# Attention statistics kept as minus the maximum, and value products of four attention steps in one burst

## The chip, the cores and the metric

The kernel runs on one core of a Trainium2 chip. The metric is the device time of one execution in microseconds (us); the figure for a kernel is the median of its runs. One execution is also profiled: its span runs from the first to the last instruction.

## The reference

Two requests, a prompt of 1024 tokens and a sample of 512, pass through two layers with the same weights, all in float32. Layer 0 (A) attends in three dilated groups (dilation 1, 4, 16) and merges them by their softmax denominators; layer 1 (B) attends in a band of 128 keys to either side, with 16 query heads over 4 key heads and a sink logit per head. Cut to what the change touches:

```python
def _dilated_group(q, k, v, dil, n_side, slopes):        # layer A, once per group
    s = einsum(qb, kb) * Dh ** -0.5
    s = where(valid, s - slopes * dil * abs(rel), -inf)
    m = max(s, -1); p = exp(s - m); den = sum(p, -1)
    o = einsum(p / den, vb); lse = m + log(den)
    ...
wts = softmax(stack(lses), axis=0)                       # merge of the groups
...
m = maximum(max(s, -1), sink)                            # layer B
p = exp(s - m); den = sum(p, -1) + exp(sink - m)
```

Before and after the attention stand the large products `u @ w_in` and `(att * silu(z)) @ w_out`, an adaLN modulation and a layer norm.

## The kernel before

**Order of the work.** The program goes through a list of projection chunks: layer A of the sample, layer A of the prompt, output layer 0, layer B of the sample, layer B of the prompt, output layer 1. A projection group is 24 matmuls into one PSUM tile `a` (line 364; every operand is split in a high and a low part, so three products for each of eight k-blocks). Inside `run_plan`, after every 4 matmuls of 512 columns or 8 of 256, `slot()` is called. `spread(tasks, slots)` makes a queue of small tasks that are handed out evenly over so many slots. So the attention of head pair `p` is threaded, task by task, between the projection matmuls of the chunks that follow. The engines take their instructions in the order in which they were written.

**An attention step** is one block of 128 queries for the two heads of a pair. It has three tasks:

- `att_a`: the score matmuls into two PSUM tiles `s` (lines 557, 558, 562; the pool has two buffers, so a step's scores wait until the step before has been read). VectorE then adds the bias, scales, and takes the row maximum in one custom instruction per head (line 412, which also writes its accumulator into the statistics `st`). One more VectorE instruction writes `nm`, the two maxima negated (line 416), and ScalarE takes the exponentials with bias `nm` and the row sums (line 419).
- `att_b`: TensorE transposes of the probabilities `P` into PSUM tiles `t` (line 430), copied to SBUF tiles `PT` by ScalarE for head 0 (line 438) and VectorE for head 1 (line 440).
- `att_c`: for a pair of steps, the value products into PSUM tile `o` (line 458): each matmul has 64 output columns of the array, head 0 in rows 0 to 63 of `o` and head 1 in 64 to 127. Then one `copy` of 128x256 (helper at lines 160 and 162, ScalarE and VectorE in turn) out of `o`. The pool of `o` has one buffer.

`pipeline` writes the tasks of a pair's 4 or 8 steps: for each i, `att_b` of step i-2, `att_a` of step i, and on even i from 4 on `att_c` of the pair that began at step i-4. Layer A runs this twice per head pair (dilations 4 and 16 together, then dilation 1), layer B once.

**Merge.** `merge_tasks` (lines 731 to 748) turns the maxima and sums in `st` into factors, in seven small VectorE instructions and one exponential. In layer B the other side of the merge is the sink logits `sinks`.

**GpSimd** (POOL) splits the streamed weights into high and low part (lines 334 and 341), for all stages.

Of the kernel before, what the change touches and what calls it, by code (L numbers as in the profile page):

```python
# [10 lines left out]
F32 = mybir.dt.float32  # L11
F32R = mybir.dt.float32r
AF = mybir.ActivationFunctionType
ALU = mybir.AluOpType
# [61 lines left out]
def trunk(ctx: ExitStack, tc: tile.TileContext, x_p, x_s, c_p, c_s, w_mod, b_mod, ln_g, ln_b,  # L76
          w_in_a, w_out_a, w_in_b, w_out_b, sink_b, pat_d, id_d, y_p, y_s):
    nc = tc.nc
    PSUM = bass.MemoryType.PSUM
    const = ctx.enter_context(tc.tile_pool(name="const", bufs=1))  # L80
    wk = ctx.enter_context(tc.tile_pool(name="wk", bufs=2))
# [5 lines left out]
    ps_o = ctx.enter_context(tc.tile_pool(name="ps_o", bufs=1, space=PSUM))  # L87
# [14 lines left out]
    sinks = const.tile([128, NH], F32, name="sinks")  # L102
# [23 lines left out]
    def after(n, f):  # L126
        delayed.append((now[0] + n, f))
# [11 lines left out]
    def spread(tasks, slots):  # L139

        q = Queue(tasks, slots)
        queues.append(q)
        return q
# [13 lines left out]
    def copy(out, in_):  # L157
        turn[0] ^= 1
        if turn[0]:
            nc.scalar.activation(out, in_, AF.Copy)  # L160
        else:
            nc.vector.tensor_copy(out, in_)  # L162
# [31 lines left out]
    def load_mod(l, third, k):  # L194
        t = slabs.get()
        nc.sync.dma_start(t, w_mod[l, k * 128:(k + 1) * 128, third * D:(third + 1) * D])
        return t

    def mod_mm(ts):
        a = ps_t.tile([128, 512], F32, tag="t", name="t")  # L200
        for i in range(NK // 2):
            for par in range(2):
                for c in range(2):
                    g = 2 * c + par
                    k = 2 * i + par
                    nc.tensor.matmul(a[32 * g:32 * g + 32, :], lhsT=sc[:, k, :],  # L206
                                     rhs=ts[k][:, c * 512:(c + 1) * 512],
                                     start=(i == 0), stop=(i == NK // 2 - 1),
                                     tile_position=(0, 32 * g))
        slabs.put(*ts)  # L210
        m = wk.tile([128, 512], F32, tag="stg", name="modrow")
        nc.scalar.activation(m, a, AF.Copy)
        return m
# [189 lines left out]

    def att_a(s):
        ss = []
        nm = wk.tile([128, 2], F32, tag="nm", name="nm", bufs=4)
        s.P = []
        ts = [ps_s.tile([128, 384], F32, tag="s", name="s") for _ in range(2)]
        s.scores(ts)
        for h, t in enumerate(ts):  # L410
            p = wk.tile([128, 384], F32, tag="P", name="P", bufs=4)
            nc.vector.tensor_tensor_reduce(  # L412
                out=p[:, :s.n], in0=t[:, :s.n], in1=s.bias(h), op0=ALU.add, op1=ALU.max,
                scale=0.125, scalar=-3e38, accum_out=s.st[:, s.b, h, 0:1])
            s.P.append(p)
        nc.vector.tensor_scalar(nm, s.st[:, s.b, :, 0], -1.0, None, ALU.mult)  # L416
        for h in range(2):
            p = s.P[h]
            nc.scalar.activation(p[:, :s.n], p[:, :s.n], AF.Exp, bias=nm[:, h:h + 1],  # L419
                                 accum_out=s.st[:, s.b, h, 1:2])  # L420

    def att_b(s):
# [17 lines left out]
                    nc.vector.tensor_copy(pt[r0:r0 + n, i:j], t[r0:r0 + n, i:j])  # L440
                i = j

    def att_c(pair):

        o = ps_o.tile([128, 256], F32, tag="o", name="o")
        a, b = pair.steps
        at = {k[4]: i for i, k in enumerate(b.keys)}
        both = [(i, at[k[4]]) for i, k in enumerate(a.keys) if k[4] in at]
        ops = [(a.keys[i], slice(i, 4 + j, 3 + j - i), slice(0, 256)) for i, j in both]
        for n, s in enumerate(pair.steps):  # L450
            ops += [(k, slice(3 * n + i, 3 * n + i + 1), slice(128 * n, 128 * n + 128)) for i, k in enumerate(s.keys)
                    if i not in [x[n] for x in both]]
        fresh = [True, True]
        for m, ((_, n, r0, v, _), blocks, cs) in enumerate(ops):
            steps = range(cs.start // 128, cs.stop // 128)
            stop = not any(both or o2[2] == cs for o2 in ops[m + 1:])
            for h in range(2):
                nc.tensor.matmul(o[64 * h:64 * h + 64, cs], lhsT=v(h)[r0:r0 + n, :],  # L458
                                 rhs=pair.PT[h][r0:r0 + n, blocks, :], start=fresh[steps[0]], stop=stop)
            for x in steps:  # L460
                fresh[x] = False
        out = a.into.rearrange("p (b q) -> p b q", q=128)[:, a.b:b.b + 1:b.b - a.b]
        copy(out, o.rearrange("p (b q) -> p b q", q=128))

    class Pair:
        pass
# [1 line left out]
    def pipeline(steps):  # L468
        tasks = []
        n = len(steps)  # L470
        for i, s in enumerate(steps):
            s.first = i % 2 == 0
            if s.first:
                s.pair = Pair()
                s.pair.steps = steps[i:i + 2]
            else:
                s.pair = steps[i - 1].pair
        for i in range(n + 3):
            if 2 <= i < n + 2:
                tasks.append(lambda s=steps[i - 2]: att_b(s))  # L480
            if i < n:
                tasks.append(lambda s=steps[i]: att_a(s))
            elif i < n + 2:
                tasks.append(None)
            if i >= 4 and i % 2 == 0:
                tasks.append(lambda s=steps[i - 4]: att_c(s.pair))
        return tasks + [None]

    def load_pat(c0, n, o=0):
# [228 lines left out]
    def merge_tasks(p, r, l, st, use=None):  # L718
# [4 lines left out]
        def m1():  # L723
            a = st["st1"]
            M = wk.tile([128, nb, 2], F32, tag="M", name="M", bufs=1)
            st["dd"] = wk.tile([128, 2, nb, 2], F32, tag="dd", name="dd", bufs=1)
            if l == 0:
                other = st["st23n"][:, :, :, 0]
            else:
                other = sinks[:, 2 * p:2 * p + 2].unsqueeze(1).to_broadcast([128, nb, 2])  # L730
            nc.vector.tensor_tensor(M, a[:, :, :, 0], other, ALU.max)
            nc.vector.tensor_tensor(st["dd"][:, 0], a[:, :, :, 0], M, ALU.subtract)
            nc.vector.tensor_tensor(st["dd"][:, 1], other, M, ALU.subtract)
            nc.scalar.activation(st["dd"], st["dd"], AF.Exp)

        def m2():
# [448 lines left out]
    with tc.manual_schedule():  # L1185
        def bg_mod(l, third):
            box = {"t": []}
            tasks = [lambda k=k: box["t"].append(load_mod(l, third, k)) for k in range(NK)] + [None] * 6
            return tasks + [lambda: box.update(m=mod_mm(box["t"])), None, lambda: mod_tr(l, third, box["m"])]
# [9 lines left out]

        def start_bg():  # L1200
            nc.sync.dma_start(sinks, sink_b[0].partition_broadcast(128))
            spread([None] * 3 + bg_mod(0, 2) + bg_mod(1, 0) + bg_mod(1, 1) + bg_mod(1, 2)
                   + bg_u(0, 0) + bg_u(0, 1), 360)

# [114 lines left out]
        for k in range(NK):  # L1319
            t = ps_t.tile([128, 4, 128], F32, tag="t", name="t")  # L1320
# [11 lines left out]
        m = modT[0][:, REQ["s"], :]  # L1332
# [60 lines left out]
```

## Time and profile before

| | before |
|---|---|
| median of 3 runs | 2706.53 us (2704.96 to 2712.18) |
| the profiled execution's own time | 2706.52 us |
| its span | 2704.7 us |
| mean granted TensorE clock | 0.988 |
| value products, line 458 | 1984 records, 193.7 us busy |
| `nm`, line 416 | 288 instructions, 119.0 us busy |
| ScalarE idle until `nm` was there (line 419) | 677.9 us |

The busy time of TensorE is the union of its matmul records. A matmul's record runs on while the next has started, so a record's length is more than the time it takes in the stream; what one takes is read from the start of one row to the start of the next. A float32 value product, which is one instruction in the program, leaves two records. A row of the timeline gives the start, the length, the engine, the line, the operation, the tiles written and read, the shapes, how many were merged into the row, and in brackets how long the engine had been idle and what ended that.

### The profile page before, as it was taken

Reading aid. Unit: us, or ns where it says so; the run is one execution under the profiler, and the core shown is the slowest. Engines: PE = TensorE matmul, PEld = TensorE weight load, DVE = VectorE, ACT = ScalarE, POOL = GpSimd, SP = SyncE. Lnnn points to the kernel's source line nnn. Section 1 sums busy time; section 2 is a strip of 40 time slices with the busy share of each in tenths; the row PEclk is TensorE's granted clock in tenths of the full one; section 3 lists DMA queues with packets and bytes.
Section 4 is the critical chain, followed back from the end, with each engine's and each line's share of the span. In section 5 each row is a group of like instructions: output and inputs, shape, how many; then the busy total and the mean of one; then the engine's idle time right before and its main releaser. Section 6 shows DMA issues by size and latency. Waiting matters only on the chain.

```text
span 2704.7 us, 39461 instructions
## 1 busy us (share of the span) xinstructions
PE 2610.9 (97%) x15139; PEld 2113.0 (78%) x15139; DVE 1253.9 (46%) x2921; ACT 982.5 (36%) x2359; POOL 945.7 (35%) x662
## 2 busy tenths in 40 slices
PE   7899999999999999999999999999999899999898
PEld 4777778778888887888888888877776678777686
DVE  4533434444243425343433434356645543555666
ACT  3334345543132423233232323242345433444321
POOL 4243334344322323223223231334554531223533
PEclk9899999999999999999999999999999999999999
DMA  8354543333222222122323232335442230211453
GB/s 263 114 147 137 153 98 102 98 98 88 59 56 73 61 56 66 42 66 56 79 56 79 52 75 48 78 118 155 133 135 63 82 91 9 58 47 54 133 170 109
DMA packets 294676, 247.36 MB, mean 91 GB/s; under 512 B 29656, under 2 KB 257880, under 8 KB 294488
## 3 DMA queue, kind: packets, MB, share of 16 engines
q1 hardware_dynamic: 291160, 244.35, 32.2%
q8 instruction: 119, 1.95, 0.3%
q10 hardware_dynamic: 3328, 0.49, 0.1%
q14 instruction: 69, 0.57, 0.1%
HBM read 198.16 MB, written 25.67 MB: 83 GB/s over the span
## 4 chain that ended last, share of the span: by engine, by line
PE 80%; DVE 7%; ACT 4%; issue 3%; POOL 2%; DMA 2%; SPq 0%; ACTq 0%; DVEq 0%; POOLq 0%
PE a L364 62%; PE o L458 6%; PE t L430 5%; PE s L557 2%; PE s L558 2%; DVE nm L416 2%; PE s L562 2%; ACT P L419 1%; DVE P L412 1%; DMA s<-s 1%; POOL s L341 1%; DMA s<-g_s 1%; ACT s L531 1%; DVE s L533 1%; PE t L206 1%
## 5 line engine op out<-in xcount | busy, mean ns | idle before, releaser
L364 PE MATMUL a<-s,s 128*128 128x512 f32 (+1 forms) x9648 | 2128.2, 370 | 23.2 <-POOL s L341 4.7
L364 PEld LDWEIGHTS a<-s,s 128*128 128x128 f32 x9648 | 1615.4, 190 | 317.6 <-issue 29.7
L341 POOL TENSOR_TENSOR s<-s,s 128x1024 fp32r<-128x1024 f32 x211 | 509.7, 2417 | 525.5 <-ACT s L336 258.6
L419 ACT ACTIVATE P<-P,nm 128x256 f32<-128x256 f32 (+2 forms) x576 | 312.3, 543 | 690.4 <-DVE nm L416 677.9
L412 DVE CUSTOM_DVE_ANT_0 P<-s,bias 128x256 f32<-128x256 f32 (+2 forms) x576 | 251.6, 472 | 238.4 <-PE s L558 128.0
L334 POOL TENSOR_SCALAR s<-s 128x1024 fp32r<-128x1024 f32 x139 | 152.5, 1097 | 465.0 <-PE a L364 382.0
L430 PE MATMUL t<-ident,P 128*128 128x128 f32 x1408 | 206.6, 275 | 8.6 <-ACT P L419 3.9
L440 DVE COPY PT<-t 128x256 f32<-128x256 f32 (+3 forms) x320 | 141.7, 447 | 139.8 <-PE t L430 136.9
L533 DVE TENSOR_TENSOR s<-a,s 64x512 fp32r<-64x512 f32 x128 | 109.8, 858 | 203.6 <-ACT s L531 202.5
L430 PEld LDWEIGHTS t<-ident,P 128*128 128x128 f32 x1408 | 166.9, 140 | 44.2 <-ACT P L419 12.2
L458 PE MATMUL o<-PT,s 128*64 128x256 f32 (+1 forms) x1984 | 193.7, 328 | 1.1 <-DVE PT L440 1.1
L458 PEld LDWEIGHTS o<-PT,s 128*64 128x64 f32 x1984 | 118.8, 136 | 87.2 <-issue 49.4
L557 PE MATMUL s<-s,s 128*128 128x256 f32 (+2 forms) x512 | 148.4, 306 | 19.0 <-DVE st L412 18.6
L160 ACT ACTIVATE s<-a 128x128 f32<-128x128 f32 (+2 forms) x147 | 56.0, 407 | 267.1 <-PE a L364 267.0
L558 PE MATMUL s<-s,s 128*128 128x256 f32 (+2 forms) x512 | 144.4, 298 | 3.2 <-DMA s<-s 3.0
L438 ACT ACTIVATE PT<-t 128x256 f32<-128x256 f32 (+3 forms) x320 | 125.9, 398 | 53.1 <-PE t L430 46.9
L542 DVE TENSOR_TENSOR s<-a,s 64x512 fp32r<-64x512 f32 x80 | 77.2, 965 | 132.0 <-ACT s L540 131.0
L557 PEld LDWEIGHTS s<-s,s 128*128 128x128 f32 x512 | 97.7, 191 | 36.7 <-DVE st L412 30.0
L416 DVE TENSOR_SCALAR nm<-st 128x2 f32<-128x2 f32 x288 | 119.0, 413 | 10.0
L162 DVE COPY s<-a 128x128 f32<-128x128 f32 (+2 forms) x105 | 49.4, 491 | 146.4 <-PE a L364 140.6
L531 ACT ACTIVATE s<-a 64x512 fp32r<-64x512 f32 x128 | 100.9, 789 | 26.7 <-PE a L364 25.9
L568 DVE SCALAR_TENSOR_TENSOR s<-th,a 128x512 f32<-128x512 f32 x48 | 43.0, 897 | 143.0 <-ACT th L566 143.0
(112 smaller groups left out, 1667.9 us busy)
## 6 DMA issues: line engine op xcount, KB each, us to landing
s<-in_w_in_a_dram SPq DMA_DIRECT2D x128, 512.0 KB, 5.2
s<-in_w_mod_dram SPq DMA_DIRECT2D x48, 512.0 KB, 7.7
s<-in_w_in_b_dram SPq DMA_DIRECT2D x40, 512.0 KB, 5.5
s<-in_w_in_a_dram SPq DMA_DIRECT2D x64, 256.0 KB, 3.2
s<-s SPq DMA_DIRECT2D x64, 256.0 KB, 4.1
s<-f_p SPq DMA_DIRECT2D x48, 256.0 KB, 5.2
s<-in_x_prompt_dram SPq DMA_DIRECT2D x16, 512.0 KB, 5.7
g_p<-s SPq DMA_DIRECT2D x16, 512.0 KB, 3.4
```

The source lines that it names most:

```text
L334: nc.gpsimd.tensor_scalar(hi, t, 1.0, 1.0, ALU.mult, ALU.mult)
L341: (nc.vector if how == "fast" else nc.gpsimd).tensor_tensor(lo, t, hi.bitcast(F32), ALU.subtract)
L364: nc.tensor.matmul(a, lhsT=lhsT, rhs=rhs, start=(n == 0), stop=(n == 3 * NK - 1))
L412: nc.vector.tensor_tensor_reduce(out=p[:, :s.n], in0=t[:, :s.n], in1=s.bias(h), op0=ALU.add, op1=ALU.max, scale=0.125, scalar=-3e38, accum ...
L416: nc.vector.tensor_scalar(nm, s.st[:, s.b, :, 0], -1.0, None, ALU.mult)
L419: nc.scalar.activation(p[:, :s.n], p[:, :s.n], AF.Exp, bias=nm[:, h:h + 1], accum_out=s.st[:, s.b, h, 1:2])
L430: nc.tensor.transpose(t[0:r0 + n, i, :], s.P[h][:, c0 - r0:c0 + n], ident)
L440: nc.vector.tensor_copy(pt[r0:r0 + n, i:j], t[r0:r0 + n, i:j])
L458: nc.tensor.matmul(o[64 * h:64 * h + 64, cs], lhsT=v(h)[r0:r0 + n, :], rhs=pair.PT[h][r0:r0 + n, blocks, :], start=fresh[steps[0]], stop=stop)
L533: nc.vector.tensor_tensor(w[e][me[1 - e]], f[e](a[me[e]]), w[e][me[e]].bitcast(F32), ALU.subtract)
L557: nc.tensor.matmul(t, lhsT=q, rhs=kk, start=True, stop=False)
L558: nc.tensor.matmul(t, lhsT=q, rhs=kl, start=False, stop=True)
```

## The change

Two things are changed.

1. The custom instruction of `att_a` scales by -0.125 and takes the minimum, so that `P` holds minus the scores and `st` minus the maximum. The exponential takes scale -1 and its bias straight from `st`; `nm` and its instruction are gone. The merge takes minima and swaps its subtractions, and `sinks` is negated once after it is loaded.
2. `att_c` takes a list of pairs. With m = 4 it writes the value products of two pairs, four steps, one behind the other into one 128x512 tile `o`, and copies it once. With m = 2 it takes one pair, as before; that is so only for the 4-step pipelines of dilation 1 (the sample's). `values` holds the matmuls, which are the same. In the order of the tasks `att_c` now stands ahead of `att_b` and `att_a` of its i.

```diff
     def att_a(s):
         ss = []
-        nm = wk.tile([128, 2], F32, tag="nm", name="nm", bufs=4)
...
             nc.vector.tensor_tensor_reduce(
-                out=p[:, :s.n], in0=t[:, :s.n], in1=s.bias(h), op0=ALU.add, op1=ALU.max,
-                scale=0.125, scalar=-3e38, accum_out=s.st[:, s.b, h, 0:1])
+                out=p[:, :s.n], in0=t[:, :s.n], in1=s.bias(h), op0=ALU.add, op1=ALU.min,
+                scale=-0.125, scalar=3e38, accum_out=s.st[:, s.b, h, 0:1])
             s.P.append(p)
-        nc.vector.tensor_scalar(nm, s.st[:, s.b, :, 0], -1.0, None, ALU.mult)
         for h in range(2):
             p = s.P[h]
-            nc.scalar.activation(p[:, :s.n], p[:, :s.n], AF.Exp, bias=nm[:, h:h + 1],
+            nc.scalar.activation(p[:, :s.n], p[:, :s.n], AF.Exp, scale=-1.0, bias=s.st[:, s.b, h, 0:1],
                                  accum_out=s.st[:, s.b, h, 1:2])
...
-    def att_c(pair):
-
-        o = ps_o.tile([128, 256], F32, tag="o", name="o")
+    def att_c(pairs):
+
+        m = len(pairs)
+        o = ps_o.tile([128, 512], F32, tag="o", name="o")[:, :256 * m]
+        for i, pair in enumerate(pairs):
+            values(pair, o[:, 256 * i:256 * i + 256])
+        a, b = pairs[0].steps
+        if b.b == a.b + 1:
+            out = a.into[:, 128 * a.b:128 * a.b + 256 * m]
+        else:
+            out = a.into.rearrange("p (j i q) -> p i j q", j=2, q=128)[:, a.b:a.b + m]
+            o = o.rearrange("p (i j q) -> p i j q", i=m, j=2)
+        copy(out, o)
+
+    def values(pair, o):
+
...
-        out = a.into.rearrange("p (b q) -> p b q", q=128)[:, a.b:b.b + 1:b.b - a.b]
-        copy(out, o.rearrange("p (b q) -> p b q", q=128))
...
     def pipeline(steps):
         tasks = []
         n = len(steps)
+        m = 2 if n == 4 and steps[0].keys[0][1] == 64 else 4
...
         for i in range(n + 3):
+            if i >= 2 + m and (i - 2) % m == 0:
+                tasks.append(lambda q=[s.pair for s in steps[i - 2 - m:i - 2:2]]: att_c(q))
             if 2 <= i < n + 2:
                 tasks.append(lambda s=steps[i - 2]: att_b(s))
             if i < n:
                 tasks.append(lambda s=steps[i]: att_a(s))
             elif i < n + 2:
                 tasks.append(None)
-            if i >= 4 and i % 2 == 0:
-                tasks.append(lambda s=steps[i - 4]: att_c(s.pair))
         return tasks + [None]
...
-            nc.vector.tensor_tensor(M, a[:, :, :, 0], other, ALU.max)
-            nc.vector.tensor_tensor(st["dd"][:, 0], a[:, :, :, 0], M, ALU.subtract)
-            nc.vector.tensor_tensor(st["dd"][:, 1], other, M, ALU.subtract)
+            nc.vector.tensor_tensor(M, a[:, :, :, 0], other, ALU.min)
+            nc.vector.tensor_tensor(st["dd"][:, 0], M, a[:, :, :, 0], ALU.subtract)
+            nc.vector.tensor_tensor(st["dd"][:, 1], M, other, ALU.subtract)
...
             nc.sync.dma_start(sinks, sink_b[0].partition_broadcast(128))
+            after(24, lambda: nc.vector.tensor_scalar(sinks, sinks, -1.0, None, ALU.mult))
```

How the instructions stand on TensorE in layer B of the prompt, last head pair, at the products of the pair of steps 2 and 3. The names are the tile written and the tiles read: `a` a projection, `s` the scores, `o` the value products, `t` a transpose; the numbered `s_...` are SBUF slabs. Before:

```order
L557 MATMUL s<-s_33_19582,s_41_22556 128x384
L558 MATMUL s<-s_4_19583,s_41_22556 128x384
L364 MATMUL a<-s_7_23025,s_34_22944 128x512
L364 MATMUL a<-s_7_23025,s_24_22945 128x512
L364 MATMUL a<-s_0_23026,s_34_22944 128x512
L364 MATMUL a<-s_7_23025,s_34_22944 128x512
L458 MATMUL o<-PT,s_6_19584 64x256 x4
L458 MATMUL o<-PT,s_6_19584 64x128 x2
L458 MATMUL o<-PT,s_8_19585 64x128 x2
L364 MATMUL a<-s_7_23025,s_24_22945 128x512
```

With the change:

```order
L568 MATMUL s<-s_4_19050,s_41_21893 128x384
L364 MATMUL a<-s_3_22265,s_29_22278 128x512
L364 MATMUL a<-s_43_22266,s_27_22277 128x512
L364 MATMUL a<-s_28_22281,s_27_22277 128x512
L364 MATMUL a<-s_28_22281,s_29_22278 128x512
L469 MATMUL o<-PT,s_6_19051 64x256 x4
L469 MATMUL o<-PT,s_6_19051 64x128 x2
L469 MATMUL o<-PT,s_6_19051 64x256 x4
L469 MATMUL o<-PT,s_6_19051 64x128 x2
L469 MATMUL o<-PT,s_8_19052 64x128 x2
L364 MATMUL a<-s_26_22282,s_27_22277 128x512
```

The six instructions of steps 0 and 1 now stand directly ahead of the eight of steps 2 and 3, with no projection matmul between. Over the whole program the value products stand in 144 unbroken groups before and in 80 with the change; their number, 992, and that of every other matmul stays.

VectorE in the same layer and head pair, at the statistics of one step. Before:

```order
L412 ISA P_21865,st1_21392<-s_21859,bias_21393 128x384
L412 ISA st1_21392 128x1
L412 ISA P_21867,st1_21392<-s_21860,bias_21393 128x384
L416 TENSOR_SCALAR nm_21858<-st1_21392 128x2
L440 COPY PT_21839<-t_21881 128x384
L533 TENSOR_TENSOR s1110_22_21777<-a_21785,s1110_22_21777 64x512
```

With the change:

```order
L411 ISA P_21241,st1_20789<-s_21235,bias_20790 128x384
L411 ISA st1_20789 128x1
L411 ISA P_21243,st1_20789<-s_21236,bias_20790 128x384
L543 TENSOR_TENSOR s1110_22_21154<-a_21162,s1110_22_21154 64x512
L543 TENSOR_TENSOR s1111_5_21155<-a_21162,s1111_5_21155 64x512
L438 COPY PT_21222<-t_21260 128x384
```

The instruction that wrote `nm` is gone from between the statistics and what follows them. VectorE has 319 instructions fewer in all: 288 of `nm`, 32 of the copies out of `o`, and one more for `sinks`.

## The prediction

> **What bounds the kernel now.** I read the busy shares first, then the stretches by stage, then what TensorE waited for, then its timeline around single bursts of value products.
>
> ```profile
> PE 2610.9 (97%) x15139; PEld 2113.0 (78%) x15139; DVE 1253.9 (46%) x2921; ACT 982.5 (36%) x2359; POOL 945.7 (35%) x662
> 690.00:1740.00 1050.00, 1048.26 (x6259) 871.58 (x6258) 409.81 (x1017) 333.06 (x849) 298.95 (x181) 1.00 0.25 62
> 2010.00:2210.00 200.00, 180.36 (x986) 135.56 (x985) 112.83 (x298) 100.92 (x274) 99.37 (x86) 0.98 0.23 69
> 2210.00:2570.00 360.00, 349.02 (x2043) 279.02 (x2041) 185.34 (x513) 142.89 (x399) 111.85 (x72) 0.99 0.22 65
> ```
>
> TensorE is busy for 97% of the span; the other engines for less than half. In the stretches (columns: length, busy time of PE, PEld, DVE, ACT, POOL, granted clock, DMA share, GB/s) the prompt's layer A, 690 to 1740 us, leaves TensorE idle for 1.7 us in 1050. There nothing that makes VectorE or ScalarE faster can help; only what TensorE itself does less of. In layer B it idles more: 19.6 us of 200 beside the sample, 11.0 of 360 beside the prompt.
>
> ```profile
> PE s L557 <- DVE st L412: 18.6, 15, 5.4
> PE t L430 <- ACT P L419: 3.9, 7, 0.8
> PE t L275 <- ACT ustg L278: 3.7, 3, 1.7
> PE t L430 <- ACT PT L438: 3.2, 9, 0.4
> PE t L755 <- ACT ustg L278: 1.2, 2, 1.0
> PE o L458 <- DVE PT L440: 1.1, 1, 1.1
> ```
>
> These are TensorE's waits (us, times, longest) that end on the attention chain or on work queued behind it. Added up without the last they are 30.6 us: no change of VectorE's and ScalarE's part can return more than that and the little that the restart of the stream adds. The last row says that the products themselves wait once, for 1.1 us.
>
> **The bursts.** What does a burst of products cost TensorE beside its own matmuls? Three bursts, and projections in blocks of four:
>
> ```profile
> 2356.25 1.08 PE L364 MATMUL a<-s,s 128*128 128x512 f32 x4
> 2357.26 1.52 PE L458 MATMUL o<-PT,s 128*64 128x256 f32 x16
> 2358.71 1.21 PE L364 MATMUL a<-s,s 128*128 128x512 f32 x4
> 2359.75 0.82 PE L430 MATMUL t<-ident,P 128*128 128x128 f32 x6
> ...
> 2361.80 1.09 PE L364 MATMUL a<-s,s 128*128 128x512 f32 x4
> 2362.73 0.97 PE L430 MATMUL t<-ident,P 128*128 128x128 f32 x6
> ...
> 2449.97 1.30 PE L458 MATMUL o<-PT,s 128*64 128x256 f32 x12
> 2451.20 3.94 PE L364 MATMUL a<-s,s 128*128 128x512 f32 x16
> ...
> 110.69 1.09 PE L458 MATMUL o<-PT,s 128*64 128x128 f32 x16
> 111.71 1.20 PE L364 MATMUL a<-s,s 128*128 128x512 f32 x4
> ```
>
> Four projections after scores, with transposes behind them, take 2361.80 to 2362.73, 0.93 us. The same four with a burst behind them take 2356.25 to 2357.26, 1.01 us: entering costs 0.08. The four behind the burst take 2358.71 to 2359.75, 1.04 us: leaving costs 0.11. Inside, the burst of 16 records (two products 256 wide and two 128 wide, each for two heads and recorded twice) takes 1.45 us, that of 12 (one 128-wide product fewer) 1.23, so a 128-wide product is 0.22. The burst at 110.69 has four of them (the sample's dilations share no keys, so nothing is 256 wide) and takes 1.02 where 0.88 is work: 0.14 more. Together 0.08 + 0.14 + 0.11 = 0.33 us for each burst, whatever it holds. A second way, over the whole piece, uses the long run of the last stage:
>
> ```profile
> 2589.91 103.80 PE a L364 x456
> ```
>
> One projection is 0.228 us there. From 2356.25 to 2359.75 are 3.50 us: 8 x 0.228 = 1.82 of projections, 1.45 - 0.14 = 1.31 of products, and 0.37 left. I take 0.35 us a burst.
>
> The order of the instructions has 144 bursts before and 80 with the change, so 64 entries and exits go: 32 in the prompt's layer A (two pipelines of 8 head pairs, four bursts to two), 16 in its layer B, 8 each in the sample's first pipeline and its layer B. The sample's second pipeline keeps its 16. 64 x 0.35 = 22.4 us, all of it on the engine that sets the end. The one thing that no row shows is the joint between two pairs in one burst, where a 128-wide product is followed by a 256-wide one. It lies between nothing (inside the bursts above, products follow each other at their own length) and a whole entry and exit, 0.35. It is nearest to the change of width inside a burst, so I take nothing; between the bounds lie 22.4 and 0 us.
>
> **The instruction that negates.**
>
> ```profile
> L416 DVE TENSOR_SCALAR nm<-st 128x2 f32<-128x2 f32 x288 | 119.0, 413 | 10.0
> 2038.73 2.39 POOL L341 TENSOR_TENSOR s<-s,s 128x1024 fp32r<-128x1024 f32 x1
> 2038.84 2.31 DVE L416 TENSOR_SCALAR nm<-st 128x2 f32<-128x2 f32 x1
> 2041.18 0.61 ACT L419 ACTIVATE P<-P,nm 128x384 f32<-128x384 f32 x1 [2.39 <-DVE nm L416]
> 2042.39 0.55 ACT L278 ACTIVATE ustg<-t,modT 128x256 f32<-128x256 f32 x1
> 2042.99 0.44 PE L275 MATMUL t<-ident,s 128*128 128x128 f32 x2 [1.70 <-ACT ustg L278]
> ```
>
> 288 instructions of 413 ns, 119.0 us, leave VectorE, which is busy for 46%. None of it is on TensorE's path by itself: it is hidden behind projection matmuls. It counts where it is late. At 2038.84 a `nm` of two columns lasts 2.31 us, as long as POOL's subtraction that began just before; the exponentials, the work queued behind them on ScalarE and then TensorE's transposes are late by it, 1.70 us in the last row. The wait for `nm` gives way to one for the accumulator of the same custom instruction, and head 0's exponential no longer waits for head 1's maximum. The minimum and the negative scale are the same instruction with other constants; I price them at no difference.
>
> ```profile
> 2154.62 2.36 POOL L341 TENSOR_TENSOR s<-s,s 128x1024 fp32r<-128x1024 f32 x1
> 2154.65 2.36 DVE L731 TENSOR_TENSOR M<-st,sinks 128x8 f32<-128x8 f32 x1
> 2158.48 0.44 PE L557 MATMUL s<-s,s 128*128 128x384 f32 x1 [2.79 <-DVE st L412]
> ```
>
> But the largest of the waits, 18.6 us for `s` to be read, need not come from `nm`: here the merge's `M` is stretched to 2.36 us by the same kind of POOL instruction, the statistics stand behind it on VectorE, and TensorE idles 2.79 us. The merge keeps all seven instructions. So the gain is bounded by 30.6 us above, and below by a loss of about one such wait, 2.8 us, if the merge falls on a POOL instruction where it did not. Of the four waits that end on ScalarE, 3.9 + 3.7 + 3.2 + 1.2 = 12.0, I count a third: 4 us.
>
> **The copies.**
>
> ```profile
> L162 DVE COPY s<-o 128x256 f32<-128x256 f32 x86 | 36.4, 423 | 125.2 <-PE o L458 124.9
> L162 DVE COPY s<-a 128x512 f32<-128x512 f32 x40 | 30.9, 771 | 103.1 <-PE a L364 99.3 <-issue 3.8
> ```
>
> 128 copies of 128x256 become 64 of 128x512. By these rows two cost 0.85 and one 0.77 us: nothing to speak of. `o` is held 0.35 us longer, and the next burst that needs it stands at least four steps further on in the pipelines that are merged. The negation of `sinks` is one small instruction.
>
> **Sum.** 2706.5 (the profiled execution, span 2704.7 and 1.8 around it, which equals the median shown) - 22.4 - 4 = 2680 us.
>
> **Rivals.**
>
> *A, the joint costs what the ends cost.* If the 0.14 us inside a burst and the cost at its ends came with each pair's tiles and not with the change between kinds of matmul, one burst of two pairs would save nothing: 2706.5 - 4 = 2702 us, no change that can be told. For it: a burst's first product was not seen apart from its pair's. Against it: projections load new weights for every matmul too, and stream at 0.228 us with none of that loss. The Trainium skill, "TensorE: Matmul & The Clock Gate", Part 3, The mechanism, says that a weight load overlaps running matmuls only when its row group differs; by that rule products over all 128 rows would each pay for their load, and the overhead would stay with the matmuls, which is this rival. The busy row above is against the rule: loads over all 128 rows are busy 78% of a span in which matmuls are busy 97%. The page "TensorEngine Tiling (Array Packing)", Key Properties, says instead that changing the tiling mode drains the engine, which by the count of bursts would be the forecast. Chance 0.07.
>
> *B, the burst stands still for the youngest probabilities.* TensorE takes its instructions in order, so a burst whose `PT` is not copied holds back every projection behind it. Before, a pair's products came as the fourth task after its last transposes; now, in the 8-step pipelines, as the second: `att_b`, `att_a`, burst.
>
> ```profile
> 2305.64 0.82 PE L430 MATMUL t<-ident,P 128*128 128x128 f32 x6
> 2308.12 0.55 DVE L440 COPY PT<-t 128x384 f32<-128x384 f32 x1
> 2309.54 1.30 PE L458 MATMUL o<-PT,s 128*64 128x256 f32 x12
> 2310.30 0.49 ACT L438 ACTIVATE PT<-t 128x384 f32<-128x384 f32 x1 [0.39 <-ACT ft L757]
> ...
> 2311.80 0.82 PE L430 MATMUL t<-ident,P 128*128 128x128 f32 x6
> 2312.33 0.49 ACT L438 ACTIVATE PT<-t 128x384 f32<-128x384 f32 x1
> 2312.66 0.56 DVE L440 COPY PT<-t 128x384 f32<-128x384 f32 x1 [2.83 <-PE t L430]
> ```
>
> From 2305.64 to 2309.54 the same three things follow one another (transposes, a step's scores, a burst, with four projections between each), 3.9 us. The copies of those transposes end at 2308.67 on VectorE and 2310.79 on ScalarE, 5.15 us after they began: a burst that needed them would wait 1.25 us. Those at 2311.80 are done after 1.4 us. For it speaks that ScalarE's copy queues behind exponentials and evacuations. Against it: the older pair's products stand first and take 1.2 to 1.45 us, so the youngest copies have some 5.2 us, and `nm` no longer delays them. The point from which it decides: 80 bursts that each wait 26.4 / 80 = 0.33 us give the gain back. At 0.5 us each it is 2680 + 40 = 2720 us. Chance 0.03.
>
> *C, the shorter chain gives more.* If all the waits of the list above went, 30.6 us, the time would be 2706.5 - 22.4 - 30.6 = 2653; if half, 2669 and below. For it speaks ScalarE's 677.9 us of waiting for `nm`; against it the 1.7 us that TensorE idles in the longest stage, and the merge. Chance 0.08.
>
> That the change doesn't do what it says is excluded for the bursts: their number is read from the order of the instructions.
>
> **How the numbers follow.** The forecast has 0.82, A 0.07, B 0.03, C 0.08. The forecast's own range: 64 bursts at 0.30 to 0.38, 19 to 24 us, with -3 to +14 from the chain, gives 2668 to 2690. Toward A and B I go on to 2694; C's upper part is inside. A measurement of this kernel tells a change of about 0.3%, 8.1 us, from none, so faster means below 2698. Faster is the forecast and C, 0.90; the same is A, 0.07; slower is B, 0.03.
>
> **What would show it.** Steps right: the busy time of L364 and the products falls by some 20 us with no record fewer; in the stretch of the prompt's layer A, where TensorE idles 1.7 us, a head pair's work comes shorter by 4 x 0.35 = 1.4 us; a merged burst of 24 to 32 records is as long as its two parts less 0.14; the wait of line 419 is for `st` and far below 677.9 us. Wrong: a burst of two pairs as long as two bursts (A); a row of PE `o` waiting on `PT` of tens of us (B); PE's waits on `st` gone (C). The forecast is wrong if bursts fall to 80 and the prompt's layer A, 1050 us, does not shorten.

## The result, and the profile after

| | before | with the change |
|---|---|---|
| median | 2706.62 us | 2659.18 us (2658.78 to 2662.64) |
| ratio, 95% interval | | 0.9822 (0.981 to 0.9835) |
| span of the profiled execution | 2704.7 us | 2656.9 us |

The change saves 47.4 us. The forecast was 26.5 (2680 us, 2668 to 2694): the direction was right, and the time lies 9 us below the range, where rival C had put it (2653 if every wait of its list went).

The busy shares of the changed kernel, and the prompt's layer A in its stretches (length, then busy time and instructions of PE, PEld, DVE, ACT, POOL, the granted clock, DMA share, GB/s):

```profile
PE 2575.1 (97%) x15139; PEld 2119.1 (80%) x15139; DVE 1145.7 (43%) x2602; ACT 981.2 (37%) x2327; POOL 943.8 (36%) x662
...
690.00:1740.00 1050.00, 1050.00 (x6327) 884.53 (x6326) 375.89 (x903) 334.74 (x843) 306.45 (x185) 1.00 0.26 64
```

TensorE is still what bounds the kernel. It has the same 15139 matmul records and is busy 35.8 us less. In the prompt's layer A, where it stood still for 1.7 us of 1050 before, it now takes 6327 matmuls in the 1050 us and took 6259: 68 more, or 1050 x 68 / 6259 = 11.4 us of work. From the same projection to the same projection, the stretch that took 1050.0 us takes 1037.5.

The groups of the changed kernel by line (busy us, mean ns of one; then idle before them and what ended it):

```profile
L364 PE MATMUL a<-s,s 128*128 128x512 f32 (+1 forms) x9648 | 2118.2, 370 | 21.4 <-DVE ystg L1080 4.4 <-POOL s L341 4.0 <-DVE s L1303 3.0
L428 PE MATMUL t<-ident,P 128*128 128x128 f32 x1408 | 201.4, 273 | 1.6 <-ACT PT L436 0.8 <-issue 0.7
L469 PE MATMUL o<-PT,s 128*64 128x256 f32 (+1 forms) x1984 | 178.3, 324 | 0.0
L567 PE MATMUL s<-s,s 128*128 128x256 f32 (+2 forms) x512 | 147.4, 304 | 21.5 <-DVE st L411 21.5
...
L417 ACT ACTIVATE P<-P,st 128x256 f32<-128x256 f32 (+2 forms) x576 | 312.5, 544 | 579.6 <-DVE st L411 573.8 <-issue 2.3 <-DMA st_s<-st 2.0
```

The lines moved: the products of line 458 are now line 469, the transposes of 430 are 428, the scores of 557 are 567, and the exponentials of 419 are 417. Before, by the same view:

```profile
L364 PE MATMUL a<-s,s 128*128 128x512 f32 (+1 forms) x9648 | 2128.2, 370 | 23.2 <-POOL s L341 4.7 <-DVE ystg L1070 4.6 <-DVE s L1292 4.0
L430 PE MATMUL t<-ident,P 128*128 128x128 f32 x1408 | 206.6, 275 | 8.6 <-ACT P L419 3.9 <-ACT PT L438 3.2 <-ACT ustg L278 0.8
L458 PE MATMUL o<-PT,s 128*64 128x256 f32 (+1 forms) x1984 | 193.7, 328 | 1.1 <-DVE PT L440 1.1
```

Projections and products together are busy 2296.5 us where they were busy 2321.9: 25.4 less, with no record fewer. The transposes lose 5.2 us of busy time and 7.0 of idle time although nothing was done to them. The scores' wait for `st` did not go; it is 21.5 us where it was 18.6.

One merged burst of the changed kernel in layer B of the prompt:

```profile
2317.91 1.09 PE L364 MATMUL a<-s,s 128*128 128x512 f32 x4
2318.93 2.60 PE L469 MATMUL o<-PT,s 128*64 128x256 f32 x28
2321.47 1.20 PE L364 MATMUL a<-s,s 128*128 128x512 f32 x4
2322.50 0.82 PE L428 MATMUL t<-ident,P 128*128 128x128 f32 x6
```

It holds the 16 and 12 records of the two bursts that the prediction measured at 1.45 and 1.23 us, and takes 2321.47 - 2318.93 = 2.54 us: the two parts less 0.14, to the last digit. Entering (1.02 us for the four projections ahead) and leaving (1.03 for the four behind) cost 0.09 and 0.10 over the undisturbed 0.93, once instead of twice.

**A list of waits that was not read.** The prediction read TensorE's waits from the rows of PE, where a wait is the gap between the end of one matmul's record and the start of the next. The record's end is modelled and lies past the point at which the next could start: at the transposes that the row of line 430 counts, matmuls began 0.16 us later, beside the usual distance of their neighbours, than the gap says, and a wait below that shows no gap at all. The loads of the weights have a list of their own. Before:

```profile
PEld s L557 <- DVE st L412: 30.0, 33, 5.8
PEld t L430 <- ACT P L419: 12.2, 25, 1.2
PEld t L430 <- ACT PT L438: 6.2, 12, 0.7
PEld t L275 <- ACT ustg L278: 5.0, 3, 2.1
PEld t L755 <- ACT ustg L278: 2.1, 2, 1.5
```

and with the change:

```profile
PEld s L567 <- DVE st L411: 31.2, 28, 3.7
PEld t L765 <- ACT ustg L278: 2.2, 2, 1.1
PEld t L428 <- ACT PT L436: 1.7, 3, 1.2
PEld t L275 <- ACT ustg L278: 1.3, 2, 1.1
```

The four rows that end on ScalarE, 12.0 us by the list of PE, are 25.5 here, and 5.2 with the change. A load may wait in the shadow of a matmul, so this list is too high where the other is too low. As a third measure I took every matmul's start less the one before it, less the median of that distance for the same kinds of neighbours, and summed what was over 40 ns. For the transposes of `P` the three say 7.1, 17.3 and 18.4 us (gaps, starts, loads): the truth lies near the loads. The Trainium skill, "Perfetto Trace Analysis", section Tensor Engine Instruction (MATMUL, LD_WEIGHTS), says that the end of a matmul in a profile is estimated from the instruction's size and not observed; the 0.16 us agree with that.

This table of late starts by what TensorE was about to write is used below (us; "scores" without the 64-row ones, whose late starts are alike in the four kernels). How neighbours are grouped into kinds moves its figures by some 2 us, and those of the projections all together, but the differences between the kernels by little:

| late starts at | before | first half alone | second half alone | both |
|---|---|---|---|---|
| transposes of `P` | 17.3 | 4.5 | 21.7 | 3.3 |
| transposes of the projections' inputs (line 275 and the like) | 16.6 | 10.1 | 17.9 | 10.6 |
| scores | 29.1 | 23.2 | 30.6 | 34.3 |
| projections | 49.5 | 44.4 | 51.4 | 44.9 |
| products | 2.5 | 1.7 | 0.6 | 0.0 |

### The profile page after: what moved, and what is told of

Its sections match the earlier page's. It is cut to its first block, busy times and chain, and to the rows that moved or that the text cites. A ratio compares the mean times of both kernels' runs of the same rounds, so it can differ in the third digit from the quotient of the medians.

```text
span 2656.9 us, 38977 instructions
## 1 busy us (share of the span) xinstructions
PE 2575.1 (97%) x15139; PEld 2119.1 (80%) x15139; DVE 1145.7 (43%) x2602; ACT 981.2 (37%) x2327; POOL 943.8 (36%) x662
## 4 chain that ended last, share of the span: by engine, by line
PE 73%; DVE 3%; POOL 1%; issue 1%; ACT 1%; DMA 1%; SPq 0%; DVEq 0%; POOLq 0%; ACTq 0%
PE a L364 56%; PE o L469 6%; PE t L428 5%; PE s L567 2%; PE s L568 2%; PE s L572 1%; POOL s L341 0%; PE t L585 0%; DVE M L741 0%; DVE P L411 0%; PE t L275 0%; DVE tt L749 0%; POOL s L269 0%; DVE s L1108 0%; ACT ustg L278 0%
## 5 line engine op out<-in xcount | busy, mean ns | idle before, releaser
L417 ACT ACTIVATE P<-P,st 128x256 f32<-128x256 f32 (+2 forms) x576 | 312.5, 544 | 579.6 <-DVE st L411 573.8
L469 PE MATMUL o<-PT,s 128*64 128x256 f32 (+1 forms) x1984 | 178.3, 324 | 0.0
L567 PE MATMUL s<-s,s 128*128 128x256 f32 (+2 forms) x512 | 147.4, 304 | 21.5 <-DVE st L411 21.5
L417 ACT ACTIVATION_READ_ACCUMULATOR P<-P,st 128x1 f32 x576 | 107.6, 187 | 0.0
```

What stands on the lines that cost most here:

```text
L417: nc.scalar.activation(p[:, :s.n], p[:, :s.n], AF.Exp, scale=-1.0, bias=s.st[:, s.b, h, 0:1], accum_out=s.st[:, s.b, h, 1:2])
L567: nc.tensor.matmul(t, lhsT=q, rhs=kk, start=True, stop=False)
```

## Experiments

The theories at the start: the bursts give 22 us as forecast, and the rest, some 25, comes from the negation (its waits being larger than listed); or the negation gives the 4 us forecast and the bursts, or the two together, give far more.

**Each half alone.** The first kernel is the one before with the first half of the change (no `nm`; bursts as they were):

```diff
-                out=p[:, :s.n], in0=t[:, :s.n], in1=s.bias(h), op0=ALU.add, op1=ALU.max,
-                scale=0.125, scalar=-3e38, accum_out=s.st[:, s.b, h, 0:1])
+                out=p[:, :s.n], in0=t[:, :s.n], in1=s.bias(h), op0=ALU.add, op1=ALU.min,
+                scale=-0.125, scalar=3e38, accum_out=s.st[:, s.b, h, 0:1])
...
-        nc.vector.tensor_scalar(nm, s.st[:, s.b, :, 0], -1.0, None, ALU.mult)
...
-            nc.scalar.activation(p[:, :s.n], p[:, :s.n], AF.Exp, bias=nm[:, h:h + 1],
+            nc.scalar.activation(p[:, :s.n], p[:, :s.n], AF.Exp, scale=-1.0, bias=s.st[:, s.b, h, 0:1],
```

with the merge and `sinks` as in the change.

> The kernel before with the first half of the change alone: statistics held as minus the maximum, the negating instruction gone; 144 bursts and their places in the order of tasks as before. The full change measured 2659.2 us against 2706.6; 64 bursts fewer at 0.36 us, as its trace again shows them, are 23 of those 47.4, so 24 us need a cause. Theory T1, the shorter chain behind the statistics gives all 24: 2682 us (2678 to 2687), and the transposes' waits for ScalarE fall as in the full change. Theory T2, the place of the bursts in the order of tasks, or the fewer tasks over the same slots, gives about 20 of them, and the chain the 4 us that were forecast: 2702 us (2699 to 2705).

The second is the changed kernel with those lines put back, `nm` and all, so that the merged bursts and the new order of the tasks are what is left.

> The second half of the change alone: bursts of two pairs and their new place among the tasks, but the maximum, its negating instruction and the exponential's wait for it as before. T1: 64 x 0.36 = 23 us less than before, 2684 us (2680 to 2688), with the transposes' waits on ScalarE as before the change. T2: the 23 and another 20, 2663 us (2660 to 2668). If the two halves need each other (neither alone shows the 24), e1 is 2702 and this one 2684.

The two others keep the new order of the tasks but give each pair its own burst again, once with `nm` and once without:

```diff
-        m = 2 if n == 4 and steps[0].keys[0][1] == 64 else 4
+        m = 2
```

> Like the run with bursts alone, but every burst holds one pair (144 bursts, as before); what is left of the change is that the products stand ahead of the transposes and the scores of their turn. T1: 2706 us (2702 to 2710), no change. T2 in its form of the order: 2687 us (2683 to 2691). T2 in its form of fewer tasks over the same slots: 2706 us, since the number of tasks is that of before.

> The changed kernel with one pair in every burst: the negating instruction gone and the new order, 144 bursts. Against the full change it prices the merging of the bursts: by the bursts' 0.36 us, 64 x 0.36 = 23 us more than it, 2682 us (2679 to 2686), by both theories on the order. If fewer tasks over the same slots matter beside the bursts, it is more than that: up to 2702 us.

Measured beside 2704.17 us of the kernel before:

| | with `nm` | without `nm` |
|---|---|---|
| old order, 144 bursts | 2704.17 | 2677.06, ratio 0.9904 (0.9889 to 0.9919) |
| new order, 144 bursts | 2706.21, ratio 1.0008 (0.9999 to 1.0017) | 2683.89, ratio 0.9921 (0.9906 to 0.9935) |
| new order, 80 bursts | 2686.50, ratio 0.9939 (0.9926 to 0.9951) | 2659.18 (beside 2706.62) |

Without `nm` the kernel is 22 to 27 us faster in every row: the negation was the larger half. Merging the bursts at the new order is worth 19.7 us with `nm` and 24.7 without it, where 22.4 were forecast for 64 bursts. Against the kernel before, the second half as a whole is worth 17.7, and on top of the first half 17.9. The last entry was measured beside other runs of the kernel before than the rest; by the ratios, the differences that use it are some 2 to 4 us larger (merging without `nm` 26.8, no `nm` in the last row 31.7, the second half on top of the first 22.2). The two halves alone add up to 44.8, close to the 47.4 of both: they do not depend much on one another.

Where the first half's time comes from is in the table of late starts: 12.8 us less at the transposes of `P`, 6.5 at the other transposes, 5.9 at the scores, 5.1 at the projections. Over all groups the late starts are some 32 us less, about the difference of the two spans (2704.7 to 2671.9; this execution was 3 us below its kernel's median). In the list of its weight loads' waits

```profile
PEld s L555 <- DVE st L411: 24.8, 35, 5.0
...
PEld t L275 <- ACT ustg L278: 1.8, 1, 1.8
...
PEld t L428 <- ACT ustg L278: 0.9, 1, 0.9
```

no transpose waits for `P` or for ScalarE's `PT`. And the prompt's layer A gains nearly nothing by this half, as the prediction said of it:

```profile
690.00:1740.00 1050.00, 1050.00 (x6272) 874.24 (x6271) 372.85 (x906) 336.95 (x848) 300.48 (x182) 1.00 0.25 63
```

13 matmuls more than before in the 1050 us, 2.2 us, where the full change has 68. The bursts give their part there, `nm` gave its part in layer B. The lengths of three stretches, each from the same projection to the same projection in every kernel (us), show it:

| stretch (its place before) | before | first half alone | second half alone | both |
|---|---|---|---|---|
| prompt's layer A (690 to 1740) | 1050.0 | 1047.2 | 1039.6 | 1037.5 |
| layer B beside the sample (2010 to 2210) | 200.1 | 186.8 | 200.1 | 194.2 |
| layer B beside the prompt (2210 to 2570) | 359.9 | 350.9 | 352.3 | 343.6 |

In layer B beside the sample, both halves together are 7.4 us slower than the first alone. What stands behind that is told below, with the empty tasks.

The two kernels with the new order and single bursts show rival B. What TensorE waited for, with `nm`:

```profile
PE o L471 <- ACT PT L438: 17.0, 14, 2.2
PE s L569 <- DVE st L412: 12.4, 9, 4.2
```

and without it:

```profile
PE s L567 <- DVE st L411: 13.1, 10, 3.4
...
PE o L469 <- DVE PT L438: 3.7, 6, 0.8
```

Where each pair has its own burst at the new place, the burst does stand still for its youngest `PT`, for 17.0 us in all with `nm` and 3.7 without it. With `nm`, what the order saves at the scores is eaten up by it. In the merged bursts the row is gone (0.0 us of idle time before line 469): the older pair's products, which stand first, cover the copies of the younger.

**Is it the wait or the instruction?** Taking out `nm` takes away 119.0 us of VectorE and a wait of ScalarE. This kernel is the changed one with the instruction put back, and nobody reads its result. By theory W the wait counts and nothing is lost; by theory Q the place in VectorE's queue counts and most of the 27 us come back.

```diff
             s.P.append(p)
+        nm = wk.tile([128, 2], F32, tag="nm", name="nm", bufs=4)
+        nc.vector.tensor_scalar(nm, s.st[:, s.b, :, 0], -1.0, None, ALU.mult)
         for h in range(2):
```

> The changed kernel with an instruction of the removed kind put back on VectorE at its old place (128x2, negates the two statistics), whose result nobody reads. The first half of the change alone gave 27 us. Theory W (the wait): the exponentials on ScalarE stood behind it, and with them the copies out of PSUM that the transposes wait for. Then VectorE's time for it is hidden, and this kernel is as fast as the changed one, 2659 to 2663 us. Theory Q (VectorE's queue): what counts is that VectorE is held, up to 2.3 us beside a subtraction on POOL, and its own copies and statistics with it. Then the 27 us come back, 2680 to 2688 us.

2659.74 us, ratio 0.9820 (0.98 to 0.984): the time of the changed kernel. The row of `nm` (count; least, median and largest ns) in the kernel before

```profile
L416 DVE TENSOR_SCALAR nm<-st x288: 168/170/2307, 95.2 to 2572.3; 128x2 f32<-128x2 f32 x144
```

in this kernel

```profile
L416 DVE TENSOR_SCALAR nm<-st x288: 169/170/2368, 95.0 to 2526.0; 128x2 f32<-128x2 f32 x144
```

and in the one with the second half alone, where it is read, with those who waited for it or for the exponentials that read it (us, times):

```profile
L416 DVE TENSOR_SCALAR nm<-st x288: 168/169/2291, 93.5 to 2554.5; 128x2 f32<-128x2 f32 x144
...
  ACT P L419: 694.0, 253
  PEld t L430: 10.9, 20
```

Unread, it is stretched beside POOL just as far, up to 2368 ns for two columns, and costs nothing. Of this instruction only the awaited stretch is paid for. Theory Q falls for it; that a stretched instruction never holds back what stands behind it on VectorE is not shown, and the merge below does just that.

**The stretch or the step in the chain?** Two things make the awaited `nm` dear: 38 of its 288 last over 1 us beside a POOL instruction before the change, and even an undisturbed one is one more step between two engines, which starts head 0's exponential only when head 1's maximum is there. In the next kernel, which has the second half alone, `nm` is made by another instruction:

```diff
-        nc.vector.tensor_scalar(nm, s.st[:, s.b, :, 0], -1.0, None, ALU.mult)
+        nc.vector.tensor_reduce(nm, s.st[:, s.b, :, 0:1], mybir.AxisListType.X, ALU.max, negate=True)
```

> The kernel with the bursts of two pairs and the maximum (2686.5 us), but the negation made by a reduction over one element with a negated output instead of by a multiplication with -1. It stands at the same place and ScalarE waits for it as before; whether POOL's subtractions stretch it too, its longest row will show. If they don't (longest row below 0.3 us), theory P, that it is the stretched instructions that cost, says 2663 to 2670 us; theory L, that any instruction more in the chain costs, with its hop between engines, says 2686 us (2682 to 2690). If the reduction is stretched as well, it is 2686 by both and tells nothing.

```profile
L416 DVE TENSOR_REDUCE nm<-st x288: 154/155/158, 95.5 to 2538.1; 128x2 f32<-128x2 f32 x144
```

No one of them is stretched, though 94 of them overlap an instruction of POOL, and the kernel takes 2672.80 us, ratio 0.9874 (0.9854 to 0.9894): 13.7 us less than with the other instruction, 13.6 more than without `nm` (by the ratios to the kernel before, 17.6 and 14.1). Both theories have about half. The list of weight loads tells the halves apart. With the `TENSOR_SCALAR`:

```profile
PEld t L430 <- ACT PT L438: 13.4, 26, 1.8
...
PEld t L430 <- ACT P L419: 10.9, 20, 1.5
```

and with the `TENSOR_REDUCE`:

```profile
PEld t L430 <- ACT PT L438: 10.6, 25, 1.8
...
PEld t L430 <- ACT P L419: 0.8, 2, 0.6
```

The transposes' waits for late exponentials were the stretch: 10.9 us, of which 0.8 are left without it. Their waits for a tile `t` that ScalarE has not copied out yet stay, 10.6 us, until the step itself is gone (1.7 us with the full change). Which part of that is the instruction's own 0.155 us, and which the waiting of head 0 for head 1, was not tried.

The Trainium skill, "SBUF — State Buffer", section Who interferes with whom, says that `tensor_scalar` can take the port pair that VectorE shares with GpSimd, that an instruction with two inputs in SBUF contends with GpSimd's reads, and that on trn2 `tensor_reduce` never contends. The trace agrees: 168 to 2307 ns for the one before the change, 154 to 158 for the other, and 1.72 us for the merge's two-input `M` below.

**Can the scores' waits be had too?** The largest wait that is left, 21.5 us, ends on `st`. The longest of them in the changed kernel:

```profile
2491.28 3.20 POOL L341 TENSOR_TENSOR s<-s,s 128x1024 fp32r<-128x1024 f32 x1
...
2492.78 1.72 DVE L741 TENSOR_TENSOR M<-st,sinks 128x16 f32<-128x16 f32 x1
...
2494.54 0.97 DVE L742 TENSOR_TENSOR dd<-M,st 128x16 f32<-128x16 f32 x1
...
2495.99 0.69 PE L567 MATMUL s<-s,s 128*128 128x384 f32 x1 [3.29 <-DVE st L411]
```

As in the prediction's example, the merge's small instructions are stretched beside POOL and the statistics stand behind them. In the next kernel three of the four instructions of the merge's second task in layer B (a product, a sum and the factor) go to POOL itself, its factor 0.5 to a later copy, and the third task comes three slots later. The fourth, the reciprocal between them, stays on VectorE:

```diff
+            E = nc.vector if l == 0 else nc.gpsimd
-            nc.vector.tensor_tensor(t[:, 0], dd[:, 0], st["st1"][:, :, :, 1], ALU.mult)
+            E.tensor_tensor(t[:, 0], dd[:, 0], st["st1"][:, :, :, 1], ALU.mult)
...
-                nc.vector.tensor_tensor(t[:, 0], t[:, 0], dd[:, 1], ALU.add)
+                E.tensor_tensor(t[:, 0], t[:, 0], dd[:, 1], ALU.add)
             nc.vector.reciprocal(t[:, 1], t[:, 0])
...
-                nc.vector.scalar_tensor_tensor(f[:, i].rearrange("p h b -> p b h"), dd[:, i], 0.5,
-                                               t[:, 1], ALU.mult, ALU.mult)
+                E.tensor_tensor(f[:, i].rearrange("p h b -> p b h"), dd[:, i], t[:, 1], ALU.mult)
...
-            nc.scalar.activation(ft[0:n], t[0:n, 0:128], AF.Copy)
+            nc.scalar.activation(ft[0:n], t[0:n, 0:128], AF.Copy, scale=0.5)
...
-        return [m1, None, None, m2, None, None, m3, None, m3b, None, None, m4, None, m5]
+        return [m1, None, None, m2, None, None] + [None] * (0 if l == 0 else 3) + [m3, None, m3b, None, None, m4, None, m5]
```

A second kernel puts an empty task wherever a burst was merged away, so that as many tasks are handed out over the same slots as before the change; a third has both:

```diff
             if i >= 2 + m and (i - 2) % m == 0:
                 tasks.append(lambda q=[s.pair for s in steps[i - 2 - m:i - 2:2]]: att_c(q))
+            elif i >= 4 and i % 2 == 0:
+                tasks.append(None)
```

> The changed kernel with an empty task wherever a burst was merged away, so that each pipeline has as many tasks over its slots as before the change. If the pace of the tasks has no part in the result: 2659 us (2656 to 2663). If the wider spacing of the tasks is part of the gain: up to 2670.

> The changed kernel with the second part of layer B's merge (two products or sums and the factor) moved from VectorE to POOL, its factor 0.5 moved into the copy behind it, and three empty tasks more between it and the transpose of the factors. In the changed kernel's trace TensorE still waits 21.5 us for scores' buffers, and about 11 of them stand behind these three instructions, stretched to 1 to 2.2 us beside POOL's subtractions. If what the removal of the negation taught holds (an instruction with its operands in SBUF that is stretched on VectorE costs when somebody waits behind it), those 11 us go: 2648 us (2644 to 2653). If the order on POOL, or the transpose of the factors, becomes the new wait: 2657 us or more.

> The same on top of the kernel with an empty task for each merged burst, which measured 2655.2 us. If its 4 us against the changed kernel are real and independent: 2644 us (2640 to 2650). If they were chance: as the kernel without the empty tasks, 2648.

> The changed kernel once more, on the chip of the two kernels above: 2659 us (2655 to 2663).

> The changed kernel with the empty tasks once more, beside it on the same chip. If the pace gives 4 us: 2655 us; if that was the spread between chips: 2659 us.

| | median us | ratio to before |
|---|---|---|
| the change, once more | 2656.47 | 0.9809 (0.9792 to 0.9826) |
| empty task | 2655.21 and 2653.17 | 0.9805 (0.9781 to 0.9828) and 0.9799 (0.9786 to 0.9813) |
| merge's second task on POOL | 2675.08 | 0.9877 (0.9864 to 0.9891) |
| both | 2668.77 | 0.9858 (0.9842 to 0.9873) |

Both kernels with the work on POOL missed: 2648 and 2644 to 2648 us were expected, and the first is 19 us slower than the change beside it. What TensorE waited for in that one:

```profile
PE s L567 <- DVE st L411: 22.9, 11, 4.5
PE a L364 <- DVE ystg L1080: 12.7, 3, 8.1
```

and the longest wait for `st` there:

```profile
2036.31 2.34 POOL L341 TENSOR_TENSOR s<-s,s 128x1024 fp32r<-128x1024 f32 x1
2036.35 2.33 DVE L742 TENSOR_TENSOR dd<-M,st 128x8 f32<-128x8 f32 x1
...
2039.15 0.69 PE L567 MATMUL s<-s,s 128*128 128x384 f32 x1 [4.50 <-DVE st L411]
```

The three instructions of the merge's first task stayed on VectorE and now meet the long POOL instruction themselves. The reciprocal has become a wait of its own, because it stands between two instructions of POOL:

```profile
DVE tt L756 <- POOL tt L755: 17.3, 6, 5.8
```

VectorE, with the next step's statistics behind the reciprocal, stands still until POOL comes to the sum: in the longest case from 2113.91 to 2119.75 us, and the scores at 2120.49 have then waited 3.60 us. Three of the scores' waits for `st`, 6.0 us, stand right behind such a reciprocal. And the factors of the last head pair are ready later: the output layer's first result waits 8.1 us for what hangs on them, where the whole group of these waits was 4.4 us. So this kernel tried POOL together with a round trip between the engines and a later third task. The wait for `st` is not shown to be curable in this way; moving the whole second task, or both tasks, was not tried.

The empty task brings the scores' late starts down from 34.3 and 29.5 us in the change's two profiles to 23 to 24 in its own two, and its median is 3.3 us below the change's beside it. The intervals overlap, so that it is faster is likely but not shown. Its trace says where both halves together lose against the first alone: layer B beside the sample takes 186.3 us with the empty tasks, as with the first half alone (186.8), and 194.2 with the change. Of the change's eight waits for `st` over 0.8 us there, five, 9.2 us in all, stand right behind the merge's second task, stretched on VectorE; in the other two kernels none does. So the fewer tasks over the same slots have brought the merge to a worse place there. The prompt's layer A takes 2.8 us longer with the empty tasks (1040.3 to 1037.5).

## Why the prediction was right and wrong

*What bounds the kernel, and where nothing can be gained by VectorE:* right. TensorE is busy for 97% of the span before and after, and in the prompt's layer A the first half gives 2.2 us by the count of matmuls (2.8 by the stretch's length) and the bursts the rest of 11.4 (12.5); the prediction's 32 bursts there at 0.35 us are 11.2.

*The bursts, 22.4 us:* right in mechanism and size. A merged burst is as long as its parts less 0.14 us; merging is worth 19.7 and 24.7 us at the same order; projections and products are busy 25.4 us less. Measured at the joint between the two pairs, a 256-wide product begins 0.10 us after the last record of a 128-wide one (57 times in the trace). That is just what the next 128-wide product takes to begin in the same place (0.10 us, 379 times; the 0.22 us of the prediction are the products of two heads, in four records). So the joint costs nothing, the lower of the two bounds of nothing and 0.35 us, and rival A falls. The Trainium skill, "TensorEngine Tiling (Array Packing)", Key Properties, has the drain at a change of mode, and it is the change of kind, not the number of tiles, that is paid for here: 0.33 us for the merged burst above by its ends and inside, 0.37 over the whole piece. That a drain is what costs it, no run here shows. What the prediction left out of this term is the new order of the tasks: alone it is worth nothing with `nm`, and by the medians costs 6.8 us without it (2677.06 to 2683.89; the intervals of the two still overlap). It also left out the pace: with fewer tasks over the same slots scores wait 6 to 11 us longer with both halves than with the first alone, in layer B beside the sample. So the second half brought 18 us (22 by the ratios) where its bursts brought 20 to 25.

*The negation, 4 us:* this is the term that failed: it was mis-sized. It is 27.1 us alone (and 27.3 beside the merged bursts, 2686.50 to 2659.18). The mechanism was the one named, a `nm` stretched beside POOL, late exponentials, late transposes. Three steps of the sizing failed. "Of the four waits that end on ScalarE, 3.9 + 3.7 + 3.2 + 1.2 = 12.0" took the gaps of PE for the waits; the weight loads say 25.5 for the same four. "I count a third" had no row behind it: all but 5.2 of the 25.5 went. And the stretch was priced, but not the step, which the prediction names ("head 0's exponential no longer waits for head 1's maximum") and leaves without a price: `nm` without any stretch still cost 13.6 us, of which the loads' list shows 8.9 as waits for ScalarE's copies out of `t` (10.6 against 1.7). The bound "30.6 us above" was taken from the same gaps and held only because it counted 18.6 us for `st`, of which 5.8 went with the first half alone (12.8 left) and nothing with the full change (21.5).

*"What would show it":* products and projections, the burst and layer A came as said. Line 419's wait was to be far below 677.9 us; it is 573.8 for `st`. Most of it is ScalarE being early for a step that has not come, so it measured neither the cost of `nm` nor its end, and it should not have stood as what speaks for rival C.

*Rival B* is real where each pair has a burst of its own at the new place (17.0 us with `nm`, 3.7 without), and is kept out by the merging, as the prediction argued from the older pair's 1.2 to 1.45 us.

*Rival C* came true in time and not in cause: its largest waits, those for `st`, did not go, and much of the time came from waits that its list shows too short (25.5 us by the weight loads, of which 5.2 are left). It had 0.08, which was too little: an instruction of VectorE that can be stretched 14 times over (168 to 2307 ns), in a chain read once a step, was reason to look for what its lateness does to the loads.

What stays open: why the empty tasks lengthen the prompt's layer A, how much of the step's 13.6 us is the instruction's own time and how much head 0's waiting for head 1, and what the remaining 20 us or so of waits for `st` would cost to remove.

## What to carry to other kernels

Where TensorE is nearly always busy, read its waits from the weight loads or from start to start; the gaps between matmul records are short by the modelled tail of each, here by more than half. A small instruction that another engine waits for is priced by its worst durations and by the step itself, not by its busy time, and the same instruction unread cost nothing here. Value products of another kind than the matmuls around them are worth collecting in long bursts, with the oldest data first so that the youngest has time to arrive.

## What was not expected of the hardware

- A `TENSOR_REDUCE` of two columns beside the same POOL instructions takes 154 to 158 ns in all of 288, where `TENSOR_SCALAR` takes 168 to 2307. With it in place of the other 13.7 us come back.
- 124.3 us of VectorE, 288 stretched and unstretched instructions, were added to the changed kernel in front of nobody, and it kept its time (2659.74 to 2659.18).
- Weight loads can lie idle for what TensorE's own rows do not show: 12.2 us for `P` in the loads' list, 3.9 in the matmuls'.
